# A final RMSNorm on Trainium2: one sum of squares and a split spread for the first column section, finer stores for the last

## The chip, the cores and the metric

The kernel runs on one core of one Trainium2 chip. The metric is the device time of one execution in microseconds (us). The kernel before has a median of 2160.24 us over 3 runs (2159.91, 2160.24 and 2164.37 us).

## The reference, cut to what matters

The reference is one layer of a streaming encoder for 2048 prompt tokens and 64 sample tokens with 1024 channels. The change touches its very end: the down projection of the gated MLP, the gated residual, and the final norm over the 1024 channels of each token.

```python
def rmsnorm(x, g):
    xf = x.astype(jnp.float32)
    y = xf * lax.rsqrt(jnp.mean(xf * xf, -1, keepdims=True) + EPS)
    return y * g.astype(jnp.float32)

def layer(...):
    ...
    x = x + gt2 * ((jax.nn.silu(g) * a) @ w_down)
    return x, ...

y_prompt = rmsnorm(xp, g_final)
y_sample = rmsnorm(xs, g_final)
```

All arithmetic is float32. The kernel multiplies weights and activations as a rounded part plus a rest: three products (`PASSES`) of the type fp32r for each block.

## The kernel before, in words

**Layout.** Activations stand with channels on the 128 partitions and tokens along the free axis. A residual tile `x3[n]` (in the profile `x`) holds 128 channels (n = 0 to 7) of 704 tokens. The 2112 tokens are worked in three groups of 704; the third holds the last 640 prompt tokens and the 64 sample tokens. The MLP's second half walks through the 2816 inner channels in parts; of each group the last part has six blocks of 128 and uses plain products: `down` (L2259) multiplies, `rows_add` (L2082, on VectorE, the profile's DVE) scales the product by `gt2` and adds it to `x3[n]`, and `down_end` squares the result on ScalarE (ACT, L2073) and adds the square into `ssum` on GpSimd (POOL, L2074).

**The last part of the last group.** It is cut into two sections of tokens, `ENDS` = 0 to 448 and 448 to 704. Rows n = 0 to 2 are done for both; then n = 3 to 7 for the first section, then n = 3 to 7 for the second. When the last row of a section is under way, `final_end` begins for it. It sums the squares over the channels with matmuls against a column of ones (L2006), turns the sums into factors (L1939 on DVE: mean plus epsilon; L1941 on POOL: power of -0.5), and scales. For the first section the factors lie one token to a partition, so `spread` (L2036) copies them to all partitions with matmuls of the factor column against the identity matrix `ident`; DVE then makes `y = x * factor` row by row (L2058, 128x448 each) and SyncE (SP) stores it (L2052). For the second section PE turns `x3` into tokens on partitions (L2001), and ACT (L2023) and DVE (L2025) scale by the factor on their partition, 512 channels at a time, on the way to the store (L2026). ACT also multiplies every finished row by the norm's weight in place (L2289).

**What sets the order.** In this stage PE, ACT, DVE and POOL run in the order in which the Python code issues instructions (`manual_schedule`), and each engine takes its queue strictly in order. SP issues most DMAs, also in order. `final_end` is a generator: `tick` runs it on to its next `yield` from inside `down`, every other block of three products, so the number of its `yield`s decides between which matmuls its steps stand. Weights are prepared ahead: SP loads a raw block, ACT rounds it (L429) and DVE makes the rest (L432), some products before PE takes it.

**The other two groups** use `final` in place of `final_end`; they too pass through `down_end`, and there the eighth row's square goes to POOL like the others (L2074, 128x704).

Of the kernel before, what the change touches and what calls it, by code (L numbers as in the profile page):

```python
# [9 lines left out]
F32 = mybir.dt.float32  # L10
F32R = mybir.dt.float32r
AF = mybir.ActivationFunctionType
# [4 lines left out]
P = 128  # L17
D = 1024
# [49 lines left out]
def tile_layer(ctx: ExitStack, tc: tile.TileContext, xT, vecs, cst, rst, w_mod, w_ada, w_qkou, w_v, w_pool,  # L68
# [21 lines left out]
    def m2_ps():  # L90
        return bank("m2")
# [591 lines left out]
    def fscr(dt=F32):  # L683
        if dt in ("rb", "ssum"):
            return spare[0].tile([P, FT], F32, tag=dt, name=dt)
        return spare[0].tile([P, FT], dt, tag="fscr", name="fscr", bufs=4)
# [1244 lines left out]
            x3.append(x)  # L1931
        return x3

    def stat_cols(ps, out, tiles):

        nf = sum(1 for t in tiles if t == P)
        for (a, b, n) in ((0, nf, P), (nf, len(tiles), tiles[-1])):
            if a < b:
                dve.tensor_scalar(out=out[:n, a:b], in0=ps[:n, a:b], scalar1=1.0 / D, scalar2=EPS,  # L1939
                                  op0=ALU.mult, op1=ALU.add)  # L1940
                pool.tensor_tensor(out=out[:n, a:b], in0=out[:n, a:b], in1=half[:n, :b - a], op=ALU.pow)  # L1941

    def final(o, x3, ssum, squares):
        for n in range(KD if squares else 0):
# [31 lines left out]
        if squares:  # L1976
            away(KD - 1)

    late = []

    def final_end(o, x3, sums, lo, hi):

        w = hi - lo
        tiles = [(t, min(P, hi - t)) for t in range(lo, hi, P)]
        for _ in range(3 if lo == 0 else 0):
            yield
        ps = m2_ps()
        rs = f2.tile([P, 5], F32, tag="rs", name="rs", bufs=2)
        if lo > 0:
            dve.memset(ps[:, :len(tiles)], 0.0)  # L1990
            yield
        order = [(ti, i) for ti in range(len(tiles)) for i in range(len(sums))]
        if lo > 0:
            order.sort(key=lambda c: c[1])
        if lo > 0:
            turned = [[take().t for _ in range(2)] for _ in tiles]

        def turn(ti, ks):
            t, n = tiles[ti]
            for k in ks:  # L2000
                pe.transpose(turned[ti][k // 4][:n, k % 4 * P:(k % 4 + 1) * P], x3[k][:, t:t + n], ident)  # L2001
        for ti, i in order:
            (t, n), (sq, base) = tiles[ti], sums[i]
            if lo > 0 and i and ti == 0:
                turn(0, range(4))
            pe.matmul(ps[:n, ti:ti + 1], sq[:, t - base:t - base + n], ones[:, 0:1], start=(i == 0 and lo == 0), stop=(i == len(sums) - 1),  # L2006
                      skip_group_check=lo > 0)

        if lo > 0:
            turn(1, range(4))  # L2010
            for ks in (range(4, KD - 1), (KD - 1,)):
                for ti in range(2):
                    turn(ti, ks)
            late[0](KD)
        stat_cols(ps, rs, [n for (t, n) in tiles])
        if lo > 0:
            ys = [f1.tile([P, 2, HX], F32R, tag="hx", name="y", bufs=2 * len(BN)).bitcast(F32).rearrange("p a t -> p (a t)")[:, :D]
                  for _ in tiles]
            for b in range(2):
                for ti, (t, n) in enumerate(tiles):  # L2020
                    c = slice(b * 512, (b + 1) * 512)
                    if ti == 0:
                        act.activation(ys[ti][:n, c], turned[ti][b][:n], AF.Copy, scale=rs[:n, ti:ti + 1])  # L2023
                    else:
                        dve.tensor_scalar(out=ys[ti][:n, c], in0=turned[ti][b][:n], scalar1=rs[:n, ti:ti + 1], scalar2=None, op0=ALU.mult)  # L2025
                    (nc.scalar if (b, ti) == (1, 0) else nc.sync).dma_start(out=yS[ti, :n, c], in_=ys[ti][:n, c])  # L2026
            yield
            return
        for _ in range(3):
            yield  # L2030

        def spread():

            pb = m2_ps()
            for ti, (t, n) in enumerate(tiles):
                pe.matmul(pb[:, t - lo:t - lo + n], rs[:n, ti:ti + 1].broadcast_to([n, P]), ident[:n, :n], start=True, stop=True)  # L2036
            return pb
        pb = spread()

        YG = ((0, 1), (1, 3), (3, 5), (5, 6), (6, 7), (7, 8))  # L2040
        y = {}
        for (a, b) in YG:
            if a % 2 == 0 or b - a == 2:
                t = f1.tile([P, 2, HX], F32R, tag="hx", name="y", bufs=2 * len(BN)).bitcast(F32).rearrange(
                    "p a t -> p (a t)")[:, :3 * w].rearrange("p (k t) -> p k t", t=w)
                j = 0
            for k in range(a, b):
                y[k] = (t, j)
                j += 1

        def store(a, b):
            nc.sync.dma_start(  # L2052
                out=yT[a:b, :, o.t0 + lo:o.t0 + hi].rearrange("k p t -> p k t"), in_=y[a][0][:, y[a][1]:y[a][1] + b - a, :w])

        def rows(upto):
            while due and due[0] < upto:
                k = due.pop(0)
                dve.tensor_tensor(out=y[k][0][:, y[k][1], :w], in0=x3[k][:, lo:hi], in1=pb[:, :w], op=ALU.mult)  # L2058
                for (a, b) in YG:
                    if b == k + 1:  # L2060
                        store(a, b)
        due = list(range(KD))
        late.append(rows)
        for k in range(KD - 1):
            rows(k + 1)
            yield

    def fsq_acc(ssum, src, lo, hi, first, adds=pool):
        if first:
            act.activation(ssum[:, lo:hi], src, AF.Square)  # L2070
        else:
            s = fscr()
            act.activation(s[:, lo:hi], src, AF.Square)  # L2073
            adds.tensor_tensor(out=ssum[:, lo:hi], in0=ssum[:, lo:hi], in1=s[:, lo:hi], op=ALU.add)  # L2074
# [117 lines left out]
    for o in fgroups:  # L2192
        Bo = B[o.g]
        held = None
        for pi, part in enumerate(PARTS[o.g]):
# [76 lines left out]
            def down_end(n, bks, secs):  # L2272
                for bk, (lo, hi) in zip(bks, secs):
                    rows_add(o, n, lo, hi, bk)
                    give(bk)
                if not lastp or nf == 2:
                    return
                lo, hi = secs[0][0], secs[-1][1]
                if ends and n == KD - 1:
                    sq7 = fscr()  # L2280
                    for (a, b, s) in o.segs:
                        a, b = max(a, lo), min(b, hi)
                        if a < b:
                            act.activation(sq7[:, a - lo:b - lo], x3[n][:, a:b], AF.Square)
                    sums.append((sq7, lo))
                else:
                    fsq_acc(ssum, x3[n][:, lo:hi], lo, hi, n == 0)
                if ends:
                    act.activation(x3[n][:, lo:hi], x3[n][:, lo:hi], AF.Copy, scale=V[:, V_GF + n:V_GF + n + 1])  # L2289

# [134 lines left out]
```

## Time and profile before

| what | value |
|---|---|
| median of 3 runs (lowest, highest) | 2160.24 us (2159.91, 2164.37) |
| the profiled execution: its own time | 2159.38 us |
| the profiled execution: span from first to last instruction | 2157.6 us |
| mean granted TensorE clock over the span | 0.999 |
| busy share of the span: PE, DVE, ACT, POOL | 99%, 76%, 51%, 12% |
| last matmul block of the down projection begins to last record | 2143.43 to 2157.6 us |

Starts are microseconds from the span's first instruction. In the views PE is TensorE's matmul, PEld its weight load, a `q` behind an engine's name its sequencer. A row of the timeline gives the start, the time from the first to the last of the instructions merged into it, engine, source line, operation, `output<-inputs`, shapes and the count; in brackets the idle time before and what ended it. The profiled execution's time is 1.78 us more than its span.

### The profile page before, as it was taken

Reading aid. Unit: us, or ns where it says so; the run is one execution under the profiler, and the core shown is the slowest. Engines: PE = TensorE matmul, PEld = TensorE weight load, DVE = VectorE, ACT = ScalarE, POOL = GpSimd, SP = SyncE. Lnnn points to the kernel's source line nnn. Section 1 sums busy time; section 2 is a strip of 40 time slices with the busy share of each in tenths; the row PEclk is TensorE's granted clock in tenths of the full one; section 3 lists DMA queues with packets and bytes.
Section 4 is the critical chain, followed back from the end, with each engine's and each line's share of the span. In section 5 each row is a group of like instructions: output and inputs, shape, how many; then the busy total and the mean of one; then the engine's idle time right before and its main releaser. Section 6 shows DMA issues by size and latency. Waiting matters only on the chain.

```text
span 2157.6 us, 38151 instructions
## 1 busy us (share of the span) xinstructions
PE 2141.4 (99%) x13570; PEld 2037.1 (94%) x13570; DVE 1645.3 (76%) x3051; ACT 1103.0 (51%) x2190; POOL 258.3 (12%) x473
## 2 busy tenths in 40 slices
PE   8999999999999999999999999999999999999999
PEld 7888888888899999999999999999999999999998
DVE  5777768678675779788698778988876597887874
ACT  4554335234323557465566445655655365565554
POOL 0010000001000301010001220100101321111112
PEclk9999999999999999999999999999999999999999
DMA  8987997897799589797669986666678675555542
GB/s 322 327 314 240 313 325 249 279 324 268 243 294 303 199 277 314 246 337 250 220 226 315 337 312 202 227 225 203 220 230 278 213 261 185 170 175 189 170 164 84
DMA packets 296551, 541.09 MB, mean 251 GB/s; under 512 B 25728, under 2 KB 112256, under 8 KB 296360
## 3 DMA queue, kind: packets, MB, share of 16 engines
q1 hardware_dynamic: 286456, 514.26, 71.2%
q10 hardware_dynamic: 9904, 24.38, 2.9%
q8 instruction: 107, 1.75, 0.3%
q14 instruction: 84, 0.69, 0.1%
HBM read 412.56 MB, written 125.98 MB: 250 GB/s over the span
## 4 chain that ended last, share of the span: by engine, by line
PE 92%; DVE 4%; DMA 2%; issue 1%; ACT 1%; SPq 0%; POOL 0%; DVEq 0%; POOLq 0%; ACTq 0%
PE mm L1633 37%; PE mm L496 24%; PE mm L2259 10%; PE mm L2113 10%; PE mm L1171 3%; DVE wt L432 1%; DMA wt<-wsum 1%; PE m L1361 1%; PE m L1383 1%; DMA hl_kept<-wt 1%; PE m L1381 1%; PE m L1346 1%; DMA mx<-xT 0%; PE mm L1107 0%; DVE x L2082 0%
## 5 line engine op out<-in xcount | busy, mean ns | idle before, releaser
L1633 PE MATMUL mm<-hx,wt 128*128 128x352 f32 x5544 | 885.9, 321 | 1.7 <-DVE wt L432 0.9
L1633 PEld LDWEIGHTS mm<-hx,wt 128*128 128x128 f32 x5544 | 878.3, 188 | 3.9 <-DVE wt L432 2.4
L496 PE MATMUL mm<-hl,wt 128*128 128x512 f32 (+2 forms) x1920 | 385.2, 356 | 0.0
L432 DVE TENSOR_TENSOR wt<-raw,wt 128x512 fp32r<-128x512 f32 (+1 forms) x460 | 310.0, 680 | 77.7 <-ACT wt L429 76.5
L429 ACT ACTIVATE wt<-raw 128x512 fp32r<-128x512 f32 (+1 forms) x460 | 274.1, 603 | 166.1 <-PE mm L496 50.2
L496 PEld LDWEIGHTS mm<-hl,wt 128*128 128x128 f32 x1920 | 314.9, 188 | 46.6 <-issue 3.6
L2113 PE MATMUL mm<-av,wt 128*128 128x352 f32 x1512 | 247.4, 323 | 1.3 <-DVE x L2082 0.7
L2113 PEld LDWEIGHTS mm<-av,wt 128*128 128x128 f32 x1512 | 242.3, 188 | 3.9 <-DVE wt L432 2.0
L2259 PE MATMUL mm<-av,wt 128*128 128x448 f32 (+1 forms) x1440 | 231.4, 322 | 0.0
L2082 DVE SCALAR_TENSOR_TENSOR x<-mm,MOD,x 128x352 f32<-128x352 f32 (+3 forms) x368 | 171.4, 505 | 77.0 <-PE mm L2259 62.0
L2259 PEld LDWEIGHTS mm<-av,wt 128*128 128x128 f32 x1440 | 220.8, 188 | 9.7
L1681 ACT ACTIVATE mm<-mm 128x352 f32<-128x352 f32 x204 | 91.4, 448 | 239.0 <-PE mm L1633 175.1
L496 PE MATMUL mm<-mx,wt 128*128 128x512 f32 (+1 forms) x960 | 182.6, 352 | 0.0
L496 PEld LDWEIGHTS mm<-mx,wt 128*128 128x128 f32 x960 | 159.3, 188 | 22.5
L1611 DVE SCALAR_TENSOR_TENSOR ta<-ea,V,ta 128x704 f32<-128x704 f32 (+1 forms) x132 | 125.7, 952 | 60.4 <-ACT ta L1606 56.3
L1611 DVE SCALAR_TENSOR_TENSOR tg<-eg,V,tg 128x704 f32<-128x704 f32 (+1 forms) x132 | 125.6, 952 | 52.9 <-ACT tg L1606 50.3
L432 DVE TENSOR_TENSOR wt<-wt 128x512 fp32r<-128x512 f32 x204 | 138.5, 683 | 11.0 <-ACT wt L429 10.8
L429 ACT ACTIVATE wt<-wt 128x512 fp32r<-128x512 f32 x204 | 124.1, 622 | 30.1 <-DMA wt<-wsum 28.7
L1589 POOL COPY ea<-UC 128x2 f32<-128x2 f32 x66 | 34.3, 520 | 537.1 <-DVE ta L1611 416.2
L1829 ACT ACTIVATE tg<-tg 128x704 f32<-128x704 f32 (+1 forms) x66 | 52.4, 794 | 71.2 <-DVE tg L1611 71.2
L1171 PE MATMUL mm<-wt,hl 128*128 128x256 f32 (+1 forms) x576 | 71.2, 284 | 0.0
L1171 PEld LDWEIGHTS mm<-wt,hl 128*128 128x128 f32 x576 | 70.2, 189 | 0.8 <-issue 0.6
(310 smaller groups left out, 2207.2 us busy)
## 6 DMA issues: line engine op xcount, KB each, us to landing
wt<-wsplit SPq DMA_DIRECT2D x132, 512.0 KB, 4.3
raw<-w_up SPq DMA_DIRECT2D x198, 256.0 KB, 4.1
wt<-hl_kept SPq DMA_DIRECT2D x96, 512.0 KB, 6.3
wt<-wsum SPq DMA_DIRECT2D x132, 256.0 KB, 4.9
wsplit<-wt SPq DMA_DIRECT2D x66, 512.0 KB, 5.1
w<-w_up SPq DMA_DIRECT2D x88, 256.0 KB, 4.4
wsum<-w SPq DMA_DIRECT2D x44, 512.0 KB, 5.7
Bd<-fscr ACTq DMA_DIRECT2D x56, 352.0 KB, 4.0
```

Source lines behind the costliest of these rows:

```text
L429: act.activation(u.w[:, 0, :u.n], u.raw[:, :u.n], AF.Copy)
L432: dve.tensor_tensor(out=u.w[:, 1, :u.n], in0=u.raw[:, :u.n], in1=u.w[:, 0, :u.n].bitcast(F32), op=ALU.subtract)
L496: pe.matmul(ps[bi][:, :hi - lo], U[:, a, k % 4 * P:(k % 4 + 1) * P], mv[k][:, b, lo:hi], start=(at == 0 and pi == 0), stop=(k == order[-1] ...
L1171: pe.matmul(ps[ti][:n, :cols], h[4 * kh + k4][:, b, lo:lo + n], U[:, a, k4 % 2 * cols:(k4 % 2 + 1) * cols], start=(kh == 0 and k4 == 0 and ...
L1589: pool.tensor_copy(ext[:, 0:2], UC[:, f, :])
L1611: dve.scalar_tensor_tensor(out=t[:, :E], in0=ext[:, j:j + E], scalar=wc(j, f), in1=t[:, :E], op0=ALU.mult, op1=ALU.add)
L1633: pe.matmul(bk.t[:, :FH], U[:, a, kc * P:(kc + 1) * P], Bo.at(nm, kc, b), start=(first and kc == 0 and pi == 0), stop=(kc == 3 and pi == 2 ...
L1681: act.activation(to.t[:, :FH], bk.t[:, :FH], AF.Copy)
L1829: act.activation(self.tg[:, :E], self.tg[:, :E], AF.Silu)
L2082: dve.scalar_tensor_tensor(out=x3[n][:, a:b], in0=bk.t[:, a - lo:b - lo], scalar=gt2(n, s), in1=x3[n][:, a:b], op0=ALU.mult, op1=ALU.add)
L2113: pe.matmul(bk.t[:, :FH], U[:, a, c:c + P], quad.put(op, m, b), start=(first and m == 0 and pi == 0), stop=(m == 1 and pi == 2), skip_grou ...
L2259: pe.matmul(bks[i].t[:, :hi - lo], U[:, a, k % 4 * P:(k % 4 + 1) * P], av[k][:, b, lo:hi], start=(k == 0 and (a, b) == PASSES[0]), stop=(k ...
```

## The change

Five edits, all in `stat_cols`, `final_end` and `down_end`.

1. The square of the eighth row is added into `ssum` for the first section too (before, it stayed in a tile of its own and was summed over by four more matmuls), and in all three groups this eighth addition is made on DVE in place of POOL. The second section of the last group keeps its tile of its own.
2. In the first section one power over 128x4 takes the place of two (128x3 and 64x1); the factors stand in the longer-lived tile `RF`, whose rows outside the 64-token tile hold the factors of the group before.
3. The factors are spread in another way: ACT rounds them to fp32r (`rh`), DVE takes the rest (`rl`), four DVE products put each onto the diagonal of identity blocks (`fscr`), and two matmuls of ones by these tiles, 128x448 fp32r each, take the place of four float32 products with the identity.
4. The numbers of `yield`s (`YA`, `YB`, `YC`, and one loop shorter by one row) set these steps elsewhere among the matmuls, and the last rows' `y` elsewhere among DVE's work.
5. The second section's result is scaled and stored in pieces of 256, 256 and 512 channels for each of its two token tiles, in place of 512 and 512: six stores for four, and ACT issues two of them.

```diff
--- before.py
+++ after.py
@@ -1931,14 +1931,17 @@
             x3.append(x)
         return x3
 
-    def stat_cols(ps, out, tiles):
+    def stat_cols(ps, out, tiles, whole=False):
 
         nf = sum(1 for t in tiles if t == P)
         for (a, b, n) in ((0, nf, P), (nf, len(tiles), tiles[-1])):
             if a < b:
                 dve.tensor_scalar(out=out[:n, a:b], in0=ps[:n, a:b], scalar1=1.0 / D, scalar2=EPS,
                                   op0=ALU.mult, op1=ALU.add)
-                pool.tensor_tensor(out=out[:n, a:b], in0=out[:n, a:b], in1=half[:n, :b - a], op=ALU.pow)
+                if not whole:
+                    pool.tensor_tensor(out=out[:n, a:b], in0=out[:n, a:b], in1=half[:n, :b - a], op=ALU.pow)
+        if whole:
+            pool.tensor_tensor(out=out[:, :len(tiles)], in0=out[:, :len(tiles)], in1=half[:, :len(tiles)], op=ALU.pow)
 
     def final(o, x3, ssum, squares):
         for n in range(KD if squares else 0):
@@ -1976,16 +1979,16 @@
         if squares:
             away(KD - 1)
 
-    late = []
+    late, YA, YB, YC = [], 3, 2, 3
 
     def final_end(o, x3, sums, lo, hi):
 
         w = hi - lo
         tiles = [(t, min(P, hi - t)) for t in range(lo, hi, P)]
-        for _ in range(3 if lo == 0 else 0):
+        for _ in range(YA if lo == 0 else 0):
             yield
         ps = m2_ps()
-        rs = f2.tile([P, 5], F32, tag="rs", name="rs", bufs=2)
+        rs = f2.tile([P, 5], F32, tag="rs", name="rs", bufs=1) if lo > 0 else RF
         if lo > 0:
             dve.memset(ps[:, :len(tiles)], 0.0)
             yield
@@ -2011,32 +2014,40 @@
             for ks in (range(4, KD - 1), (KD - 1,)):
                 for ti in range(2):
                     turn(ti, ks)
+            late[0](KD - 1)
+        stat_cols(ps, rs, [n for (t, n) in tiles], lo == 0)
+        if lo > 0:
             late[0](KD)
-        stat_cols(ps, rs, [n for (t, n) in tiles])
-        if lo > 0:
             ys = [f1.tile([P, 2, HX], F32R, tag="hx", name="y", bufs=2 * len(BN)).bitcast(F32).rearrange("p a t -> p (a t)")[:, :D]
                   for _ in tiles]
-            for b in range(2):
+            for c0, c1 in ((0, 256), (256, 512), (512, D)):
                 for ti, (t, n) in enumerate(tiles):
-                    c = slice(b * 512, (b + 1) * 512)
+                    src = turned[ti][c0 // 512][:n, c0 % 512:c0 % 512 + c1 - c0]
                     if ti == 0:
-                        act.activation(ys[ti][:n, c], turned[ti][b][:n], AF.Copy, scale=rs[:n, ti:ti + 1])
+                        act.activation(ys[ti][:n, c0:c1], src, AF.Copy, scale=rs[:n, ti:ti + 1])
                     else:
-                        dve.tensor_scalar(out=ys[ti][:n, c], in0=turned[ti][b][:n], scalar1=rs[:n, ti:ti + 1], scalar2=None, op0=ALU.mult)
-                    (nc.scalar if (b, ti) == (1, 0) else nc.sync).dma_start(out=yS[ti, :n, c], in_=ys[ti][:n, c])
+                        dve.tensor_scalar(out=ys[ti][:n, c0:c1], in0=src, scalar1=rs[:n, ti:ti + 1], scalar2=None, op0=ALU.mult)
+                    (nc.scalar if ti == 0 and c0 else nc.sync).dma_start(out=yS[ti, :n, c0:c1], in_=ys[ti][:n, c0:c1])
             yield
             return
-        for _ in range(3):
-            yield
-
-        def spread():
-
-            pb = m2_ps()
-            for ti, (t, n) in enumerate(tiles):
-                pe.matmul(pb[:, t - lo:t - lo + n], rs[:n, ti:ti + 1].broadcast_to([n, P]), ident[:n, :n], start=True, stop=True)
-            return pb
-        pb = spread()
-
+        nt = len(tiles)
+        rh, rl = (f2.tile([P, 8], F32R, tag=nm, name=nm) for nm in ("rh", "rl"))
+        for _ in range(YB):
+            yield
+        act.activation(rh[:, :nt], rs[:, :nt], AF.Copy)
+        dve.tensor_tensor(out=rl[:, :nt], in0=rs[:, :nt], in1=rh[:, :nt].bitcast(F32), op=ALU.subtract)
+        dg = [fscr(F32R) for _ in range(2)]
+        for d, r in zip(dg, (rh, rl)):
+            for i, j in ((0, nt - 1), (nt - 1, nt)):
+                n = tiles[i][1]
+                v = d[:, tiles[i][0]:tiles[j - 1][0] + n].rearrange("p (t c) -> p t c", c=n)
+                dve.tensor_tensor(out=v, in0=ident[:, :n].unsqueeze(1).broadcast_to([P, j - i, n]),
+                                  in1=r[:, i:j].bitcast(F32).unsqueeze(2).broadcast_to([P, j - i, n]), op=ALU.mult)
+        for _ in range(YC):
+            yield
+        pb = m2_ps()
+        for i, d in enumerate(dg):
+            pe.matmul(pb[:, :w], ones_r, d[:, :w], start=i == 0, stop=i == 1)
         YG = ((0, 1), (1, 3), (3, 5), (5, 6), (6, 7), (7, 8))
         y = {}
         for (a, b) in YG:
@@ -2061,7 +2072,7 @@
                         store(a, b)
         due = list(range(KD))
         late.append(rows)
-        for k in range(KD - 1):
+        for k in range(KD - 2):
             rows(k + 1)
             yield
 
@@ -2276,7 +2287,7 @@
                 if not lastp or nf == 2:
                     return
                 lo, hi = secs[0][0], secs[-1][1]
-                if ends and n == KD - 1:
+                if ends and n == KD - 1 and lo > 0:
                     sq7 = fscr()
                     for (a, b, s) in o.segs:
                         a, b = max(a, lo), min(b, hi)
@@ -2284,7 +2295,7 @@
                             act.activation(sq7[:, a - lo:b - lo], x3[n][:, a:b], AF.Square)
                     sums.append((sq7, lo))
                 else:
-                    fsq_acc(ssum, x3[n][:, lo:hi], lo, hi, n == 0)
+                    fsq_acc(ssum, x3[n][:, lo:hi], lo, hi, n == 0, dve if n == KD - 1 else pool)
                 if ends:
                     act.activation(x3[n][:, lo:hi], x3[n][:, lo:hi], AF.Copy, scale=V[:, V_GF + n:V_GF + n + 1])
```

TensorE, from the end of the first section's matmuls to the spread (lines L2259 and L2270 are the down projection, L2006 and L2009 the sums of squares, L2036 and L2050 the spread). Before:

```order
L2259 MATMUL mm<-av,wt 128x256 x24
L2006 MATMUL m_23350<-ones_r,ssum 128x1
L2006 MATMUL m_23350<-ones_r,fscr 128x1
L2006 MATMUL m_23350<-ones_r,ssum 128x1
L2006 MATMUL m_23350<-ones_r,fscr 128x1
L2006 MATMUL m_23350<-ones_r,ssum 128x1
L2006 MATMUL m_23350<-ones_r,fscr 128x1
L2006 MATMUL m_23350<-ones_r,ssum 64x1
L2006 MATMUL m_23350<-ones_r,fscr 64x1
L2259 MATMUL mm<-av,wt 128x256 x18
L2036 MATMUL m_23388<-V,rs 128x128 x3
L2036 MATMUL m_23388<-V,rs 128x64
```

The same place with the change:

```order
L2270 MATMUL mm<-av,wt 128x256 x24
L2009 MATMUL m_23351<-ones_r,ssum 128x1 x3
L2009 MATMUL m_23351<-ones_r,ssum 64x1
L2270 MATMUL mm<-av,wt 128x256 x30
L2050 MATMUL m_23405<-fscr,ones_r 128x448 x2
L2270 MATMUL mm<-av,wt 128x256 x36
```

Eight sums are four, the spread is two products for four, and it stands 30 matmuls behind the sums, where 18 stood between.

VectorE, behind the spread: `y` is the first section's result, `x3` to `x7` inside the second section are its residual rows, each added in two pieces (192 prompt tokens and 64 sample tokens). Before:

```order
L2058 TENSOR_TENSOR y_23393<-x0_19179,m2_23388 128x448
L2058 TENSOR_TENSOR y_23394<-x1_19181,m2_23388 128x448
L2058 TENSOR_TENSOR y_23394<-x2_19183,m2_23388 128x448
L2082 SCALAR_TENSOR_TENSOR x5_19189<-mm_8742,MOD_108,x5_19189 128x192
L2082 SCALAR_TENSOR_TENSOR x5_19189<-mm_8742,MOD_108,x5_19189 128x64
L2058 TENSOR_TENSOR y_23395<-x3_19185,m2_23388 128x448
L2058 TENSOR_TENSOR y_23395<-x4_19187,m2_23388 128x448
L2058 TENSOR_TENSOR y_23395<-x5_19189,m2_23388 128x448
L2082 SCALAR_TENSOR_TENSOR x6_19191<-mm_8738,MOD_108,x6_19191 128x192
```

With the change:

```order
L2069 TENSOR_TENSOR y_23408<-x0_19179,m2_23405 128x448
L2093 SCALAR_TENSOR_TENSOR x5_19189<-mm_8742,MOD_108,x5_19189 128x192
L2093 SCALAR_TENSOR_TENSOR x5_19189<-mm_8742,MOD_108,x5_19189 128x64
L2069 TENSOR_TENSOR y_23409<-x1_19181,m2_23405 128x448
L2069 TENSOR_TENSOR y_23409<-x2_19183,m2_23405 128x448
L2069 TENSOR_TENSOR y_23410<-x3_19185,m2_23405 128x448
L2093 SCALAR_TENSOR_TENSOR x6_19191<-mm_8738,MOD_108,x6_19191 128x192
```

Six rows of `y` stood ahead of `x6`, four stand there now; `x5` moved from behind the third to behind the first.

VectorE, at the end of the second group of tokens (`x_14340` is its eighth residual row; the `wt` behind it is the rest of a weight block of the third group). The difference there:

```order
+L2093 SCALAR_TENSOR_TENSOR x_14340<-mm,MOD,x_14340 128x448
+L2093 SCALAR_TENSOR_TENSOR x_14340<-mm,MOD,x_14340 128x256
+L2085 TENSOR_TENSOR ssum<-ssum,fscr 128x704
 L432 TENSOR_TENSOR wt<-raw,wt 128x512
 L1939 TENSOR_SCALAR RF<-m_18641 128x5
```

The first two rows only have a new line number; the addition is new on this engine and stands ahead of the weight block, and it needs ACT's square of the row above it. The first group's end has the same addition ahead of `L1693 TENSOR_TENSOR qs<-qs`.

## The prediction

> **What bounds the kernel now.** I read the page first, then the chain of waits from 2050 us on, then the timeline of the last 20 us.
>
> ```profile
> PE 2141.4 (99%) x13570; PEld 2037.1 (94%) x13570; DVE 1645.3 (76%) x3051; ACT 1103.0 (51%) x2190; POOL 258.3 (12%) x473
> ```
>
> TensorE sets the pace everywhere but at the edges, so the edit can only move PE's own instructions, or the end, where PE is no longer the last. The chain of waits (start, us, what):
>
> ```profile
> 2140.16 2.31 PE mm L2259 x18
> 2142.47 1.04 PE m L2036 x8
> ...
> 2143.54 1.68 DVE y L2058 x3
> 2145.22 0.54 DVE x L2082 x2
> 2145.76 1.59 DVE y L2058 x3
> 2147.35 0.53 DVE x L2082 x2
> ...
> 2147.96 0.43 ACT fscr L2073
> ...
> 2148.52 0.75 POOL ssum L2074
> 2149.27 1.88 issue
> ```
>
> From 2143.54 on it is not PE: six rows of `y` and two residual additions on DVE, then x6's square on ACT and its addition on POOL, hold the second section's sum. The timeline says how closely PE follows:
>
> ```profile
> 2138.44 0.28 PE L2006 MATMUL m<-ones_r,ssum 128*128 128x1 f32 x2
> ...
> 2140.09 2.38 PE L2259 MATMUL mm<-av,wt 128*128 128x256 f32 x18
> 2140.20 0.22 DVE L1939 TENSOR_SCALAR rs<-m 128x3 f32<-128x3 f32 x2 [1.65 <-PE m L2006]
> 2142.31 1.19 PE L2036 MATMUL m<-V,rs 128*128 128x128 f32 x8
> 2143.43 5.90 PE L2259 MATMUL mm<-av,wt 128*128 128x256 f32 x48
> 2147.26 0.60 DVE L2082 SCALAR_TENSOR_TENSOR x<-mm,MOD,x 128x192 f32<-128x192 f32 x2
> 2149.32 0.52 PEld L2006 LDWEIGHTS m<-ones_r,ssum 128*128 128x128 f32 x4 [0.19 <-POOL ssum L2074]
> 2151.92 1.27 ACT L2023 ACTIVATE y<-mm,rs 128x512 f32<-128x512 f32 x2 [0.99 <-POOL rs L1941]
> 2152.64 1.31 SPq L2026 DMA_DIRECT2D yS<-y  x3
> ```
>
> PE had to wait for POOL's `ssum` for 0.19 us only: matmuls and DVE's chain end together. An edit that shortens one of them alone gains no more than that. Behind it lies a fixed ladder: x6's addition at 2147.26, the sum 2.06 us later, the scaling 2.60 us behind that, the first store 0.72 us on.
>
> **TensorE.** The eight sums are 16 passes and reach from 2138.44 to 2140.09, 1.65 us. Half stay; by passes that saves 0.8. The addition they need instead now runs on DVE:
>
> ```profile
> 2136.61 0.58 ACT L2284 ACTIVATE fscr<-x 128x448 f32<-128x448 f32 x1 [2.32 <-DVE x L2082]
> 2137.94 0.61 DVE L2082 SCALAR_TENSOR_TENSOR x<-mm,MOD,x 128x192 f32<-128x192 f32 x2 [1.43 <-PE mm L2259]
> 2139.14 0.73 POOL L2074 TENSOR_TENSOR ssum<-ssum,fscr 128x256 f32<-128x256 f32 x1 [4.26 <-ACT fscr L2073]
> ```
>
> The square ends at 2137.19, DVE is idle until 2137.94 (1.43 us free), and one 128x448 row costs it 0.5 to 0.6 (the three `y` above, 1.68): done by 2137.85, before PE's 2138.44. That idle stretch hides it; without it the 0.6 would delay the sums. The spread takes from 2142.31 to 2143.43, 1.12 us; two fp32r products of 448 columns cost 0.17 to 0.2 each by this row:
>
> ```profile
> 2127.83 10.78 PE L2259 MATMUL mm<-av,wt 128*128 128x448 f32 x63
> ```
>
> (10.78/63 = 0.17), so 0.4: saves 0.7. In all PE ends its matmuls 1.5 us earlier, at about 2147.6 for 2149.1. This is not yet the end's gain.
>
> **When the spread can start.** PE resumes at 2139.3 (0.8 earlier); 30 matmuls at 2.22/18 = 0.123 us put the spread at 2143.0, its second product at 2143.1. DVE gets the sums at 2139.4. The power of four columns waits for the POOL addition that ends at 2139.87. Its price:
>
> ```profile
> L1404 POOL TENSOR_TENSOR sf<-sf,half x20: 542/1009/1452, 84.3 to 717.4; 128x4 f32<-128x4 f32 x16, 64x1 f32<-64x1 f32 x4
> L724 DVE TENSOR_TENSOR scr<-V,RS x2: 415/417/419, 607.3 to 611.7; 128x256 f32<-128x256 f32 x2
> L724 DVE TENSOR_TENSOR fscr<-V,RF x2: 840/840/841, 1253.5 to 1705.0; 128x640 f32<-128x640 f32 x2
> ```
>
> Median 1.01, longest 1.45; I take 1.01, since DVE does nothing then but wait for the result. [...]
>
> So the power ends at 2140.9. ACT's rounding of 128x4 costs about 0.2 (an estimate: below its 0.42 for 128x256 in the chain). DVE's rest costs 0.16 to 0.2 (nearest the two L1939 rows, 0.22 together), and the four diagonal products, by the L724 rows, about 0.55 for 384 columns and 0.2 for 64, 1.5 one after another, 1.2 if they overlap as the `y` do. That ends at 2142.5 to 2142.95 with the semaphores, 0.15 to 0.6 us before PE's second product. Tight, but I let PE not wait. x4's addition, behind the products on DVE, is then due 2142.6 to 2143.2; before it was 2141.81, but only x4's square follows.
>
> **The chain that sets the end.** The first `y` starts at 2143.5 as before: the spread's end moves by less than 0.1. What changes is the order. Before, six `y` and one residual pair stood between the spread and x6: 1.61 + 0.52 + 1.59 = 3.72 us. Now four `y` at 0.53 and one pair, 2.65. So x6 starts at 2146.15, 1.1 us earlier. By the ladder PE sums at 2148.2, 0.6 us after its last matmul, and the scaling starts at 2150.8: **minus 1.1 us**. x7 comes at 2147.8, 1.6 earlier, and doesn't bind: its sum stands behind x6's in PE's queue. Of `y`, the last is behind the second factors' step on DVE and ends by 2150.6, before the scaling.
>
> **The stores.** A first piece of 256 is scaled in 0.42 to 0.48 in place of 0.69, so its store can be issued 0.24 us earlier. But the end is the transfer:
>
> ```profile
> 1252.00:1253.00 1.00, 1.00 (x9) 1.00 (x7) 0.39 (x1) 0.22 (x1) 1.00 (x1) 1.00 1.03 347
> 2154.00:2156.00 2.00, 0.00 (x0) 0.00 (x0) 0.00 (x0) 0.00 (x0) 0.00 (x0) 0.59 1.05 406
> ...
> 2153.22 0.34 ACTq L2026 DMA_DIRECT2D yS<-y  x1
> ```
>
> Of the first two rows, stretches of the trace, the last two columns are the DMA engines' share and GB/s: saturated at 406 while 2 KB rows leave, at 347 where all packets are 1 KB (256 channels). Of the 1 MB, half now goes in 1 KB rows: 0.52/347 against 0.52/406 is 1.51 against 1.29, 0.22 more. ACT issues between its scalings, 0.34 each, so its last 512 channels leave about 0.6 later than before, which the backlog covers as long as 2.6 us of transfer are queued. Bounds minus 0.24 and plus 0.3; I take minus 0.05. [...]
>
> **The two earlier groups.** DVE's new 128x704 addition (0.84 to 0.95 by the 640-column row and one like it) waits for ACT's square.
>
> ```profile
> 1248.81 0.42 DVE L1693 TENSOR_TENSOR qs<-qs 128x256 f32<-128x256 f32 x1 [2.72 <-DMA qs<-w_quad]
> ...
> 1697.59 0.68 DVE L432 TENSOR_TENSOR wt<-raw,wt 128x512 fp32r<-128x512 f32 x1
> ...
> 1697.76 0.79 ACT L2073 ACTIVATE fscr<-x 128x704 f32<-128x704 f32 x1 [0.60 <-DVE x L2082]
> ...
> 1698.30 0.33 SPq L408 DMA_DIRECT2D raw<-w_up  x1
> ...
> 1703.04 5.03 PE L1633 MATMUL mm<-hx,wt 128*128 128x352 f32 x30
> ```
>
> In the first it falls into 2.72 us of idle time ahead of `qs`. In the second, the weight rest that ran at 1697.59 now runs at 1699.5, 1.9 late, and SP's raw load, released by it at 1698.30, is issued at 1700.2. PE takes that weight six matmuls into the row at 1703.04, at 1704.0: 3.8 us of cover remain. Cost nothing; without cover, up to 1.9 each.
>
> **Sum.** Minus 1.1 and minus 0.05: minus 1.15 us. The profiled execution took 2159.38 (span 2157.6 and 1.78 around it), which becomes 2158.2; the median of 2160.24 lies 0.86 above it and becomes **2159.1 us**, 0.05% faster. A measurement of this kernel can tell about 0.2% (4.3 us) from no change; this is a quarter of it.
>
> **Rivals.**
> - *The diagonals come late* (0.15). For: six small steps over three engines between sums and spread, 0.15 us of slack in the worse bound. Against: the rows' own overlaps. If the power takes 1.45 and nothing overlaps, PE and the first `y` stand 0.5 us: minus 0.6, 2159.6.
> - *x6's chain doesn't bind* (0.12). If POOL keeps up, PE's 1.5 us come through, and the stores their 0.24: minus 1.75, 2158.5. Against: the DVE row counts above.
> - *The store drains no sooner* (0.08). If ACT's issues hold its last scaling longer than the backlog lasts, or a `yT` store is still under way, 1.1 is lost at the end: 2160.2.
> - *Slower: DVE's addition starves PE in the earlier groups* (0.07). Price 1.9 us at each boundary; it decides once the weight rest is over 3.8 us late, for instance if POOL's seventh addition runs late and DVE waits for it. Against: that addition is a row early. One stall leaves plus 0.75, 2161.0; both, plus 2.65, 2162.9.
>
> My forecast keeps 0.58. **Range 2157.2 to 2161.3 us**: the cases from 2158.5 to 2161.0 and about 1 us for the median, which in three runs had one of 2164.37. All cases lie within 0.2%; for such a run in the median, and for what I have not seen, faster 0.03, within 0.94, slower 0.03.
>
> **What would show it.** Right: four sums of about 0.85 us; the spread at 2143.0 with no wait before it; x6's addition at about 2146.2; PE idle about 0.6 us ahead of the second sums, released by POOL; the scaling at 2150.8. Wrong: PE waiting for DVE's diagonal at the spread; PE waiting for `wt` after 1703; over 0.3 us between the end of one store's data and the next; a last record before 2155.5 or after 2157.4.

## The result, and the profile after

The change makes the kernel slower by a little: a median of 2165.32 us (22 runs, 2160.32 to 2171.8) against 2161.88 us for the kernel before on the same chip (22 runs, 2158.66 to 2165.64). The ratio is 1.0014, with a 95% interval of 1.0008 to 1.002. The forecast was 2159.1 us, and 2157.2 to 2161.3.

| what | before | after |
|---|---|---|
| the profiled execution: its own time | 2159.38 us | 2163.84 us |
| its span | 2157.6 us | 2162.0 us |
| first sums of the first section begin (PE) | 2138.44 us | 2144.11 us |
| second section's sums begin (PE) | 2149.32 us | 2153.93 us |
| scaling begins to last record | 5.7 us | 5.6 us |

The third row is the surprise. When the first instruction that the last group's edits touch starts, the kernel is already 5.67 us late. From there on it gains: at the second sums 4.61 us are left, so the end became 1.06 us shorter. First the end, then the 5.67 us.

The busy row of the page after:

```profile
PE 2145.1 (99%) x13556; PEld 2038.8 (94%) x13556; DVE 1650.6 (76%) x3060; ACT 1102.3 (51%) x2192; POOL 256.7 (12%) x470
```

PE has 14 instructions less and is busy 3.7 us longer. The chain of waits after (start, us, what):

```profile
2144.27 0.77 PE m L2009 x8
2145.04 3.76 PE mm L2270 x30
2148.80 0.42 PE m L2050 x2
...
2149.24 0.62 DVE y L2069
2149.86 0.52 DVE x L2093 x2
2150.38 1.59 DVE y L2069 x3
2151.97 0.53 DVE x L2093 x2
...
2153.15 0.73 POOL ssum L2085
2153.87 1.74 issue
```

The chain runs over the same engines as before, with four `y` and one residual pair ahead of x6 in place of six and one. The timeline after (start, length, engine, line, operation; in brackets the idle time before and what ended it):

```profile
2142.93 0.62 DVE L2085 TENSOR_TENSOR ssum<-ssum,fscr 128x448 f32<-128x448 f32 x1 [0.77 <-ACT fscr L2084]
...
2144.11 0.93 PE L2009 MATMUL m<-ones_r,ssum 128*128 128x1 f32 x8
...
2144.97 3.83 PE L2270 MATMUL mm<-av,wt 128*128 128x256 f32 x30
...
2145.49 1.02 POOL L1944 TENSOR_TENSOR RF<-RF,half 128x4 f32<-128x4 f32 x1
2146.54 0.20 ACT L2037 ACTIVATE rh<-RF 128x4 fp32r<-128x4 f32 x1 [1.28 <-POOL RF L1944]
2146.78 0.16 DVE L2038 TENSOR_TENSOR rl<-RF,rh 128x4 fp32r<-128x4 f32 x1 [1.48 <-ACT rh L2037]
2146.86 0.69 DVE L2044 TENSOR_TENSOR fscr<-V,rh 128x384 fp32r<-128x384 f32 x2
2147.46 0.69 DVE L2044 TENSOR_TENSOR fscr<-V,rl 128x384 fp32r<-128x384 f32 x2
...
2148.64 0.57 PE L2050 MATMUL m<-fscr,ones_r 128*128 128x448 f32 x2
...
2149.04 4.48 PE L2270 MATMUL mm<-av,wt 128*128 128x256 f32 x36
...
2151.89 0.60 DVE L2093 SCALAR_TENSOR_TENSOR x<-mm,MOD,x 128x192 f32<-128x192 f32 x2
...
2153.93 0.52 PEld L2009 LDWEIGHTS m<-ones_r,ssum 128*128 128x128 f32 x4 [0.62 <-POOL ssum L2085]
...
2156.39 0.84 ACT L2027 ACTIVATE y<-mm,rs 128x256 f32<-128x256 f32 x2 [1.33 <-POOL rs L1942]
```

Shifted by 5.67 us, every step here stands within 0.1 us of where the prediction put it, or inside the bounds that it gave. The new wait is the foreseen one: PE idles 0.62 us ahead of the second sums.

The 5.67 us come from instructions that the change does not touch. PE's groups by shape (line, operation, count, then busy us and mean ns of one, then idle time), before:

```profile
L1633 PE MATMUL mm<-hx,wt 128*128 128x352 f32 x5544 | 885.9, 321 | 1.7 <-DVE wt L432 0.9 <-ACT mm L1681 0.8
L2113 PE MATMUL mm<-av,wt 128*128 128x352 f32 x1512 | 247.4, 323 | 1.3 <-DVE x L2082 0.7 <-DVE wt L432 0.5
L2259 PE MATMUL mm<-av,wt 128*128 128x448 f32 x720 | 157.1, 363 | 0.0
L2259 PE MATMUL mm<-av,wt 128*128 128x256 f32 x720 | 97.4, 280 | 0.0
```

and after:

```profile
L1633 PE MATMUL mm<-hx,wt 128*128 128x352 f32 x5544 | 888.9, 321 | 1.1 <-ACT mm L1681 0.6 <-DVE wt L432 0.5
L2124 PE MATMUL mm<-av,wt 128*128 128x352 f32 x1512 | 246.6, 322 | 1.6 <-DVE x L2093 0.7 <-DVE wt L432 0.6
L2270 PE MATMUL mm<-av,wt 128*128 128x448 f32 x720 | 159.1, 366 | 0.0
L2270 PE MATMUL mm<-av,wt 128*128 128x256 f32 x720 | 98.4, 282 | 0.0
```

The counts are equal and there is no idle time in the last two rows, yet they take 2.0 and 1.0 us more (in the groups by line, where overlapping products count once, the two together have 231.4 and 234.4 us; below these are the last-part products, though two of the five parts of six blocks in which they run are earlier parts of the first group). The `hx` products take 3.0 more, the 352-column `av` products 0.8 less: plus 5.2 of the 5.67. Start to start, in the mean of all pairs that follow each other, one 448-column product takes 201.0 ns before and 203.7 ns after.

What differs for these products is where `av` lies in SBUF. No view shows an address; what follows is worked out from the tiles in the code. The change adds two tiles of 32 bytes to the right-hand pool (`rh`, `rl`) and drops one `rs` buffer, 20 bytes that are taken as 32 with padding: 32 bytes more. That pool is taken to end at a fixed address, so that every tile allocated ahead of these (`OC`, `x0` to `x7`, all buffers of `av`) slides 32 bytes down. The buffers of `av` are 5632 bytes, 22 times 256, so all have one place within 256 bytes, and after the change it is 32 lower.

### The profile page after: what moved, and what is told of

Read it like the earlier page. It is cut to its first block, busy times and chain, and to the rows that moved or that the text cites. A ratio compares the mean times of both kernels' runs of the same rounds, so it can differ in the third digit from the quotient of the medians.

```text
span 2162.0 us, 38129 instructions
## 1 busy us (share of the span) xinstructions
PE 2145.1 (99%) x13556; PEld 2038.8 (94%) x13556; DVE 1650.6 (76%) x3060; ACT 1102.3 (51%) x2192; POOL 256.7 (12%) x470
## 4 chain that ended last, share of the span: by engine, by line
PE 91%; DVE 4%; DMA 2%; issue 1%; ACT 1%; SPq 0%; POOL 0%; DVEq 0%; POOLq 0%; ACTq 0%
PE mm L1633 38%; PE mm L496 24%; PE mm L2270 11%; PE mm L2124 10%; PE mm L1171 3%; DVE wt L432 1%; PE m L1361 1%; PE m L1383 1%; PE m L1381 1%; PE m L1346 1%; DMA w<-w_ada 1%; DMA wt<-wsum 1%; DVE x L2093 1%; PE mm L1107 0%; DMA hl_kept<-wt 0%
## 5 line engine op out<-in xcount | busy, mean ns | idle before, releaser
L1633 PE MATMUL mm<-hx,wt 128*128 128x352 f32 x5544 | 888.9, 321 | 1.1 <-ACT mm L1681 0.6
L2270 PE MATMUL mm<-av,wt 128*128 128x448 f32 (+1 forms) x1440 | 234.4, 324 | 0.0
L2270 PEld LDWEIGHTS mm<-av,wt 128*128 128x128 f32 x1440 | 222.2, 188 | 11.5
```

The source lines that it names most:

```text
L1633: pe.matmul(bk.t[:, :FH], U[:, a, kc * P:(kc + 1) * P], Bo.at(nm, kc, b), start=(first and kc == 0 and pi == 0), stop=(kc == 3 and pi == 2 ...
L2270: pe.matmul(bks[i].t[:, :hi - lo], U[:, a, k % 4 * P:(k % 4 + 1) * P], av[k][:, b, lo:hi], start=(k == 0 and (a, b) == PASSES[0]), stop=(k ...
```

## The experiments

Three theories stood at the start. A: the place of the tiles changes PE's rate. B, the prediction's slower rival: DVE's addition in the two earlier groups starves PE. C: chance between executions. All kernels do the whole computation. Times are medians, each beside the kernel before on the same chip.

**1. The change with the addresses of before.** Both small tiles share one of 32 bytes:

```diff
-        rh, rl = (f2.tile([P, 8], F32R, tag=nm, name=nm) for nm in ("rh", "rl"))
+        r2 = f2.tile([P, 8], F32R, tag="rh", name="rh")
+        rh, rl = r2[:, :4], r2[:, 4:]
```

> The changed kernel with rh and rl side by side in one 32-byte tile, so that every other tile lies where it lay in the kernel before (the change had moved the whole block of the MLP's tiles down by 32 bytes). Theory A (the place of the tiles slows PE): the last part's products of 448 and 256 columns return from 203.8 and 119.8 ns a piece to the 201.0 and 117.8 of before, and the time is 1 us below before (ratio about 0.9995), 4.4 us under the changed kernel. Theory B (DVE's addition at the ends of the earlier groups starves PE): the time stays 3 to 4 us over before (1.0014). Theory C (chance of the runs): no ratio repeats.

**2. The kernel before, 32 bytes lower.** One tile that nothing uses:

```diff
+        f2.tile([P, 8], F32, tag="pad", name="pad")
```

> The kernel before with one unused 32-byte tile beside rs, so that the MLP's tiles lie 32 bytes lower, as in the changed kernel; no instruction differs. Theory A: 3.5 to 5 us slower than before (1.0016 to 1.0023), 448-column products at about 203.8 ns. Theories B and C: as before (1.0000).

**3. The change, 64 bytes lower**, by the same line put into the change:

> The changed kernel with one more unused 32-byte tile: the tiles lie 64 bytes below their old place. If theory A goes by the place modulo 64 bytes, the products are back at 201.0 ns and the time is 1 us below before; if any other place than the old one is slow, it stays 3 us or more above. Theories B and C: 3 to 4 us over before, or no order.

**4. The change without DVE's addition in the earlier groups:**

```diff
-                    fsq_acc(ssum, x3[n][:, lo:hi], lo, hi, n == 0, dve if n == KD - 1 else pool)
+                    fsq_acc(ssum, x3[n][:, lo:hi], lo, hi, n == 0, dve if ends and n == KD - 1 else pool)
```

> The changed kernel with the eighth addition of the two earlier groups back on POOL; tiles lie as in the changed kernel. Theory A: no change against the changed kernel (1.0014 of before). Theory B: the 4 us come back (0.9995).

The kernel before had 2162.27 us (27 runs). Measured: 2162.31 for the first (ratio 1.0001, 0.9989 to 1.0014), 2164.42 for the second (1.0007, 0.9998 to 1.0017), 2192.4 for the third (1.0137, 1.0122 to 1.0151), 2164.36 for the fourth (1.0004, 0.9995 to 1.0013). The groups of the first:

```profile
L1633 PE MATMUL mm<-hx,wt 128*128 128x352 f32 x5544 | 891.3, 322 | 3.3 <-DVE wt L432 1.7 <-ACT mm L1681 1.6
...
L2271 PE MATMUL mm<-av,wt 128*128 128x448 f32 x720 | 157.0, 363 | 0.0
L2271 PE MATMUL mm<-av,wt 128*128 128x256 f32 x720 | 97.3, 280 | 0.0
```

of the second:

```profile
L2260 PE MATMUL mm<-av,wt 128*128 128x448 f32 x720 | 159.0, 366 | 0.0
L2260 PE MATMUL mm<-av,wt 128*128 128x256 f32 x720 | 98.5, 282 | 0.0
```

of the third:

```profile
L1633 PE MATMUL mm<-hx,wt 128*128 128x352 f32 x5544 | 920.1, 326 | 1.4 <-ACT mm L1681 1.0 <-DVE wt L432 0.2
...
L2271 PE MATMUL mm<-av,wt 128*128 128x448 f32 x720 | 160.1, 367 | 0.0
```

and of the fourth:

```profile
L2270 PE MATMUL mm<-av,wt 128*128 128x448 f32 x720 | 159.0, 366 | 0.0
L2270 PE MATMUL mm<-av,wt 128*128 128x256 f32 x720 | 98.4, 282 | 0.0
```

An unused tile alone makes the kernel before lose what the change lost in these products; the change at the old addresses has the old values; moving the addition back to POOL alters nothing in them. B falls by the profiles: after the change PE has no wait at the two places where the prediction's slower rival puts it (1240 to 1260 and 1690 to 1770 us). The times alone are too coarse: the fourth run's interval just reaches the 0.9995 of B. A holds for the `av` products, but missed in the times: the first run was not 1 us below the kernel before, and the second was 2.2 us slower, not 3.5 to 5, with an interval that reaches 1. The third run shows that the place can cost ten times more: there the `hx` products, which don't read `av`, take 34 us more than in the kernel before.

For the 3.0 us of the `hx` products in the profile after, C is the likely cause: such differences come without the change. The view by stretches shows line 1633 alone in 840 to 860 us (stretch, its length, PE busy and products, weight loads, clock, DMA share, GB/s). The kernel before:

```profile
840.00:860.00 20.00, 20.00 (x128) 20.00 (x127) 1.00 0.94 332
```

The change:

```profile
840.00:860.00 20.00, 20.00 (x122) 20.00 (x122) 1.00 0.98 340
```

The first experiment:

```profile
840.00:860.00 20.00, 20.00 (x122) 20.00 (x121) 1.00 0.97 335
```

With no idle time and a clock of 1.00, 122 products stand where 128 were: a product takes either 158 or 167 ns for tens of microseconds on end (in the profile after 167 ns from 838 to 865 and from 1170 to 1202 us). The first experiment has such stretches too, with `av` where it was before. Over thirteen profiles with `hx` unmoved, leaving out those 64 and 224 bytes lower, this group takes 885.9 to 891.3 us; two profiles of one kernel (runs 5 and 10) have 888.1 and 891.2. The profile before is the lowest of all: the prediction started from a lucky execution.

**5 to 8. Which tile, and with what period?** P: the place of `av` within 128 bytes decides. Q: that of `x` or `OC`. R: the distance moved. Runs 5 and 6 add an unused tile of 96 or 128 bytes to the first experiment. Run 7 puts two tiles of 64 bytes around `av` in the kernel before, run 8 a third at the end:

```diff
+            if k == 4 and o is fgroups[0]:
+                f2.tile([P, 16], F32, tag="pad", name="pad")
             x = f2.tile([P, FT], F32, tag=f"x{k}", name=f"x{k}")
...
+            if k == 3 and o is fgroups[0]:
+                f2.tile([P, 16], F32, tag="low", name="low")
```

> The change with both small tiles in one of 32 bytes, and an unused tile of 96 bytes at the end of the pool: every tile of the pool lies 96 bytes lower than in the kernel before (av at 64 bytes past a multiple of 128). Theory P (the place of av within 128 bytes sets the rate of both kinds of matmuls): a fourth value of its own. The three places so far gave 201.0, 203.8 and 205.3 ns for the 448-column product and +0, +2 and +30 us in all; if the fourth closes the circle back to the first, it lies between the first and the third, so 201 to 205 ns and 0 to +30 us against the kernel before. Theory R (it is the distance that counts, not the place within 128 bytes): worse than the shift of 64 bytes, over 205.3 ns and over +30 us.

> The same with an unused tile of 128 bytes: every tile lies 128 bytes lower, so at the same place within 128 bytes as in the kernel before. Theory P: 201.0 ns for the 448-column product, the 352-column products mostly at 158 ns, and about 1 us less than the kernel before, from the end of the program, as far as the slow stretches of the 352-column products let that be seen. Theory R: over 205.3 ns and over +30 us.

> The kernel before, with two unused tiles that move the buffers of av alone 64 bytes lower (x0 to x3 and OC move by 128, x4 to x7 not at all). No instruction differs. Theory P: as with the shift of 64 bytes, so 205.3 ns for the 448-column product, 166 ns for nearly all 352-column products, +31 us against the kernel before. Theory Q (it is the residual tiles x or OC whose place matters): 201.0 ns, mostly 158 ns, no difference.

> The kernel before, with three unused tiles that move x0 to x7 and OC 64 bytes lower within 128 (x4 to x7 by 64, x0 to x3 and OC by 192), and av by 128, so to the same place within 128 bytes. No instruction differs. Theory P: 201.0 ns for the 448-column product and no difference from the kernel before. Theory Q: 205.3 ns and +31 us.

The kernel before had 2161.32 us. Run 5 gave 2156.61 us (ratio 0.9985, 0.9976 to 0.9994), run 6 2164.42 (1.0014, 1.0004 to 1.0023), run 7 2193.32 (1.015, 1.0136 to 1.0164), run 8 2163.33 (1.0012, 1.0003 to 1.0021). Groups of run 7:

```profile
L1633 PE MATMUL mm<-hx,wt 128*128 128x352 f32 x5544 | 916.6, 325 | 0.9 <-DVE wt L432 0.3 <-ACT mm L1681 0.3
...
L2263 PE MATMUL mm<-av,wt 128*128 128x448 f32 x720 | 160.1, 367 | 0.0
```

of run 6:

```profile
L2273 PE MATMUL mm<-av,wt 128*128 128x448 f32 x720 | 159.9, 367 | 0.0
L2273 PE MATMUL mm<-av,wt 128*128 128x256 f32 x720 | 96.8, 279 | 0.0
```

and of run 8:

```profile
L2265 PE MATMUL mm<-av,wt 128*128 128x448 f32 x720 | 159.9, 367 | 0.0
L2265 PE MATMUL mm<-av,wt 128*128 128x256 f32 x720 | 96.9, 279 | 0.0
```

`av` alone, 64 bytes lower, does all that the third run did; moving `x0` to `x7` does nothing (run 8 is run 6, whose `x` stand elsewhere): Q falls. But 128 bytes are not the old place: P's period is wrong. And 96 bytes beat the old place, which neither theory foresaw (P had 0 to plus 30 us): the two shapes take 156.4 and 94.7 us in run 5.

**9 to 12. The change itself at one place, and the period.** The kernel before with 96 bytes, the change with 96 bytes again, and the change with 256 and 512 bytes.

> The kernel before with one unused tile of 96 bytes at the end of the pool; no instruction differs. If the place of av alone made the 3.3 us that the last-part products lost in the change with the shift of 96 bytes: 200.1 ns for the 448-column product, 228.1 us for all last-part products in place of 231.4, and 3 to 4 us less than the kernel before in time. If instead the change's own instructions had a part in it: no less than 2 us below the kernel before is not reached.

> The change with every tile of the pool 96 bytes lower, beside the kernel before with the same 96 bytes. With av at one place in both, what is left between the two is the change itself. By the prediction's terms: 1.1 us less than the kernel before with 96 bytes, and with the place's gain 4 to 5 us less than the kernel before. If the change costs something ahead of its own instructions whatever the place: no difference, or slower than the kernel before with 96 bytes.

> The change with every tile 256 bytes lower. If what counts is the place within 256 bytes: 201.0 ns for the 448-column product, 117.4 for the 256-column one, and 1 us below the kernel before. If it is the place within a longer stretch, or the distance to another buffer: other values, and no forecast of the time inside -5 to +30 us.

> The change with every tile 512 bytes lower. If what counts is the place within 256 or within 512 bytes: 201.0 and 117.4 ns, and 1 us below the kernel before. If it is neither: other values.

The kernel before had 2162.84 us. The four: 2159.31 (ratio 0.9986, 0.9978 to 0.9995), 2157.0 (0.9981, 0.9972 to 0.999), 2160.21 (0.9988, 0.9979 to 0.9997), 2161.18 (0.9991, 0.9981 to 1.0001). With 256 and 512 bytes the 448-column product is back at 201.0 ns, the 256-column one at 117.3: **the place comes round every 256 bytes.** In run 9 the place alone gives 228.1 us for the last-part products, 3.3 less than before, and the time follows. The ends of runs 9 and 10, with `av` at one place, of the kernel before:

```profile
2138.16 0.28 PE L2008 MATMUL m<-ones_r,ssum 128*128 128x1 f32 x2
...
2149.06 0.61 PE L2008 MATMUL m<-ones_r,ssum 128*128 128x1 f32 x4
```

and of the change:

```profile
2138.97 0.93 PE L2011 MATMUL m<-ones_r,ssum 128*128 128x1 f32 x8
...
2148.76 0.61 PE L2011 MATMUL m<-ones_r,ssum 128*128 128x1 f32 x4 [0.49 <-DVE x L2096]
```

The first sums start 0.81 later, the second 0.30 earlier: 1.11 us gained, as in the profile after. In the times, the four comparisons at equal places of `av` (run 1 and the kernel before; run 10 and run 9; runs 11 and 12 and the kernel before; run 6 and run 8) differ in their means by plus 0.4, minus 1.5, minus 1.1 and plus 0.1 us; weighted by their errors, minus 0.8 with a standard error of 0.4. The forecast of minus 1.15 lies within that, and so does a gain close to none.

**13 to 16. Why do the `hx` products care?** They read `hx` and `wt`, not `av`. Distance theory: the distance from `hx` to `av` counts. Own-place theory: `av`'s place alone. In two runs a tile at the start of the other pool moves `hx` (with all of that pool):

```diff
             spare.append(fctx.enter_context(tc.tile_pool(name="f1", bufs=1)))
+            spare[0].tile([P, 16], F32, tag="low", name="low")
```

> The kernel before, with an unused tile of 64 bytes at the start of the pool that holds hx: hx lies 64 bytes higher, av where it was, so the distance from hx to av is 64 bytes shorter, as in the kernel before with av 64 bytes lower. No instruction differs. Distance theory: about 166 ns for nearly all 352-column products and about +30 us; the av products at 201.0 ns, since they read av and wt, which have not moved. Own-place theory (av's place alone): 352-column products mostly at 158 ns, no difference over 3 us. A third outcome is open: hx's own place gives the 352-column products a rate that was not seen before.

> The kernel before with av 64 bytes lower and hx 192 bytes higher, which within 256 bytes is 64 lower: their distance within 256 bytes is that of the kernel before. Distance theory: 352-column products mostly at 158 ns; in all +4 us, from the av products at 205.3 ns. Own-place theory: 166 ns and +31 us, as in the two runs with av 64 bytes lower.

> The change with every tile of the pool 160 bytes lower, av at a multiple of 256 bytes. The last-part products took 231.4, 234.4, 235.8, 228.1, 233.7 us with 0, 32, 64, 96, 128 bytes; no order is seen in these, so 228 to 236 us and -5 to +4 us in all, if the 352-column products keep their stretches; +30 us if this is a second place that slows them.

> The change with every tile 224 bytes lower, which within 256 bytes is 32 higher than in the kernel before. As for the shift of 160 bytes: 228 to 236 us for the last-part products and -5 to +4 us in all, or +30 us if this place slows the 352-column products.

The kernel before had 2160.91 us. Run 13: 2168.14 (ratio 1.0035, 1.0023 to 1.0047); run 14: 2171.32 (1.0049, 1.0036 to 1.0061); run 15: 2163.38 (1.0011, 1.0002 to 1.0019); run 16: 2185.13 (1.0111, 1.0098 to 1.0125). The `hx` group of run 13:

```profile
L1634 PE MATMUL mm<-hx,wt 128*128 128x352 f32 x5544 | 894.6, 322 | 0.5 <-DVE wt L432 0.5
```

and of run 14:

```profile
L1634 PE MATMUL mm<-hx,wt 128*128 128x352 f32 x5544 | 894.5, 322 | 0.5 <-DVE wt L432 0.5
```

Both theories fail. Once `hx` is moved by 64 or 192 bytes, its products take a third, even rate of about 160.2 ns, with no stretches at 167, whether `av` lies at its old place (run 13) or 64 bytes lower (run 14). So the 64 bytes of `av` that cost these products 30 us with `hx` at its old place cost them nothing here. Why that is stays open.

For the `av` products the two traces settle what the other runs leave open: whether `av`'s own place counts, or its distance from the weights. In the last group the weights of rows n = 3 to 7 lie in the pool of `hx` (L384 and L399 of the kernel before), so runs 13 and 14 moved them too, and "which have not moved" in the expectation of run 13 is wrong for them. These are 16 us of those rows in the first section, where only 448-column products run (the view by stretches, the down projection's line alone). The kernel before:

```profile
2119.00:2135.00 16.00, 16.00 (x81) 15.02 (x81) 1.00 0.10 26
```

Run 13, the weights 64 bytes higher and `av` unmoved:

```profile
2127.00:2143.00 16.00, 16.00 (x79) 14.62 (x79) 1.00 0.09 26
```

Run 14, the weights 192 bytes higher and `av` 64 lower, which within 256 bytes is the old distance:

```profile
2131.00:2147.00 16.00, 16.00 (x82) 15.02 (x81) 1.00 0.09 26
```

Run 7, `av` 64 bytes lower and the weights unmoved:

```profile
2153.00:2169.00 16.00, 16.00 (x80) 14.62 (x79) 1.00 0.09 26
```

Start to start, the 90 products of these rows take 200.1, 205.3, 200.4 and 205.3 ns. Weights 64 bytes up do what `av` 64 bytes down does, and with both moved alike the old rate is back. In the first two groups, whose weights lie in a pool that stood still, the product goes by `av` alone: 201.1, 201.5, 205.4 and 205.5 ns. So **the distance from `av` to its weights within 256 bytes decides**, and not `av`'s own place; in all other runs the weights stood still, and the two can't be told apart. One thing this does not explain: in run 13, twelve 448-column products of row n = 2, with `av` and weights at their old places by the code, take 206.3 ns in the mean for 201.4 before.

All places of `av` in one table (us; the last column is the median against the kernel before of the same chip; `hx` and all weights unmoved):

| `av` lower by | last-part products | `hx` products | difference |
|---|---|---|---|
| 0 (before; run 1) | 231.4; 231.2 | 885.9; 891.3 | 0; 0.0 |
| 32 (after; run 2; run 4) | 234.4; 234.4; 234.3 | 888.9; 888.8; 890.5 | +3.4; +2.2; +2.1 |
| 64 (run 3; run 7) | 235.8; 235.9 | 920.1; 916.6 | +30.1; +32.0 |
| 96 (runs 5, 10; run 9) | 228.1, 228.0; 228.1 | 888.1, 891.2; 891.1 | -4.7, -5.8; -3.5 |
| 128 (run 6; run 8) | 233.6; 233.8 | 889.2; 887.8 | +3.1; +2.0 |
| 160 (run 15) | 234.6 | 887.2 | +2.5 |
| 224 (run 16) | 229.4 | 918.3 | +24.2 |
| 256, 512 (runs 11, 12) | 231.3, 231.3 | 887.2, 890.9 | -2.6, -1.7 |

The change with 96 bytes more (runs 5 and 10) beats both kernels, in two separate comparisons.

## Why the prediction was wrong, and where it was right

**Right: the end.** The four sums take 0.86 us for 0.85. The spread starts at 2148.64 (2143.0 plus 5.67 is 2148.67), with no wait ahead of it, and PE goes on 0.40 us later, as two products of 0.2 should. The 0.17 that the prediction had as its other bound was misread: the 63 products of that row are 39 of 448 columns and 24 of 256. DVE's addition waits 0.77 us for ACT's square and ends at 2143.55, 0.56 us ahead of PE's sums. The steps between them: 1.02 for the power (1.01 forecast), 0.20 for the rounding, 0.16 for the rest, and 1.29 from the first diagonal product to the end of the last (1.2 to 1.5). During the power DVE ran nothing, as the choice of 1.01 supposed. In the profile before, of the sixteen 128x4 powers of the prediction's row (L1404) the nine during which DVE ran nothing took 1.01 us each, the seven beside DVE's instructions 1.12 to 1.45; but three 128x4 powers of other lines (L540, L560) took 1.01 beside DVE's work too, and no run shows the mechanism. x6's addition comes at 2151.89 (2146.15 plus 5.67 is 2151.82), PE waits 0.62 us (0.6), the scaling starts at 2156.39 (2156.47). Gain at the end: 1.06 and 1.11 us in two pairs of profiles, for 1.1. From the scaling to the last record the time fell from 5.7 to 5.6, for minus 0.05 forecast; the view's tenth doesn't tell more.

**Right: the two earlier groups.** DVE's longer addition cost PE no wait, as said: after the change PE waits for nothing at the ends of these groups (1240 to 1260 and 1690 to 1770 us), line 1633 waits 0.5 us for `wt` in all, less than the 0.9 before, and the fourth run shows the same products without the addition. The rival that foresaw a slower kernel had the sign, and neither its place nor its cause.

**Wrong: "so the edit can only move PE's own instructions, or the end, where PE is no longer the last".** The step reads PE's 99% as a rate that can't change unless instructions do. But here PE's time per product depends on how far its moving operand lies from its weights (448 columns of `av`: 200.0 to 205.5 ns), and the sum put this at nothing without a reason. It is plus 3.0 us for the last-part products and minus 0.8 for the 352-column `av` products, 2.2 us in all, by the groups of the second run, which holds nothing else; its time rose by 2.2 us. With the gain of 1.1 at the end that makes plus 1.1.

**Mis-sized: the base.** The sum was made from one execution of 2159.38 us, corrected by a median of three. Over 22 runs the kernel before has 2161.88. That the first profile was a fast one was luck, and it shows in the `hx` products: 885.9 us, the least of thirteen. They make 3.0 of the 4.5 us between the two profiled executions. The rest closes: 3.0 + 2.2 and some 0.4 in other groups, less 1.06, is 4.5.

**What stays open.** The terms give plus 1.1 us; the medians differ by 3.4 us, and the ratio is plus 3.0 us, with an interval of 1.7 to 4.3. By means alone, the second run's plus 2.2 (standard error 0.6) less the 0.8 (0.4) of the end is plus 1.4, and 1.6 short of the change's 3.0 (0.6), with a standard error of 1.0: that can be scatter, or a term that is missing. The stretches of the `hx` products are large enough for it, but no run shows that the change makes them more frequent.

## What to carry to other kernels

Compare first the instructions that a change does not touch: if identical matmuls with no idle time take longer, look up where their operands and weights lie. A new tile, here of 32 bytes and used only at the end, can move the others of its pool; hold the addresses when an edit of a microsecond is to be judged, here by putting two tiles into one or by padding to 256 bytes. Where matmuls fill 99% of the span, trying the places of an operand within 256 bytes can be worth more than an edit like this one: with the kernel before, 96 bytes lower gave minus 3.5 us and 64 bytes lower plus 32.0.

## What the runs showed of the hardware

- The rate of the last part's fp32r products depends on the distance from their moving operand to their weights within 256 bytes: 201.0, 203.7, 205.5, 200.0, 205.0, 203.5, 202.2 ns start to start for 448 columns with `av` 0, 32, 64, 96, 128, 160 and 224 bytes lower. 256 and 512 bytes give the first value again, and run 9 has the value of runs 5 and 10 with another program. Moving the weights in place of `av` (run 13), or both alike (run 14), shows that it is the distance. All moves were multiples of 32 bytes; the eighth such place was not tried, and no run shows the mechanism.
- The 352-column `hx` products have two rates, 158 and 167 ns, at a clock of 1.00 and without idle time, for tens of microseconds on end and at other times in another execution. With `av` 64 or 224 bytes lower they keep the second for most of the program (916.6 to 920.1 us for the group, in place of 885.9 to 891.3); with `hx` moved they have one rate, about 160.2 ns (runs 13 and 14). No run shows the mechanism.
